# Dilated convolution on one core: which eight image rows go through four DMA engines alone

## The chip, the core and the metric

The kernel runs on one core of one Trainium2 chip. The core has a matrix engine (TensorE, "PE" in the profile, with its weight loads as "PEld"), a vector engine (VectorE, "DVE"), a scalar engine (ScalarE, "ACT"), GpSimd ("POOL") and a sync engine ("SP"). All data moves between the chip's main memory and the on-chip memory (128 partitions) through 16 DMA engines; in this kernel every transfer is issued from SP's queue. The metric is the device time of one execution in microseconds (us). Of several executions the median is taken: 126.56 us before the change, of 3 runs from 126.53 to 126.76.

## The reference

A 3x3 convolution with dilation 2 and padding 2 over 16 images of 64 channels and 64x64 pixels, giving 128 channels:

```python
batch, c_in, h, w, c_out, k, dilation = 16, 64, 64, 64, 128, 3, 2
x_pad = np.pad(x, ((0, 0), (0, 0), (pad, pad), (pad, pad)), mode='constant')   # pad = 2
for kh in range(k):
    for kw in range(k):
        output[b, co] += weight[co, ci, kh, kw] * x_pad[b, ci, kh*dilation:kh*dilation+h, kw*dilation:kw*dilation+w]
```

Input and output are float32: 16.8 MB come in and 33.6 MB go out.

## The kernel before

**Tiling.** Two images make a pair: their 2 x 64 input channels fill the 128 partitions, and there are 8 pairs. A pair is worked on in four groups of 16 image rows (`GR`), so that the main loop runs over 32 groups, `G` = 0 to 31, with `pb` the pair and `g` the group in it. The output of a pair stands in a ring of three slots (`o_ring`, L69): in a slot, partition = output channel, and then 64 rows of 64 pixels for image 0 of the pair (`m` = 0) and the same for image 1.

**Arithmetic of a group.** Input rows are cast to float16 (L83, L85), and adjacent row blocks are added (L95). Row sums, even blocks and odd blocks go through TensorE into psP, psA and psB (L186). ScalarE copies psP out of the accumulators (L248); VectorE adds it to psA and to psB and writes the result to the ring (L254). Once the second of these adds is through, all 16 rows of the group are in the ring for both images.

**Loads and stores, in SP's order.** SP issues everything itself, one transfer after the other, and each DMA engine takes its share of them in that order:

- weights; pair 0 in two pieces; pairs 1 and 2; all before the loop;
- at the end of group 0: the load of pair 3 (the fourth load, L65), and behind it the early store of the top rows of image 0 (L267 before);
- at the end of group 2 the load of pair 4, of group 3 that of pair 5, and then the two stores of pair 0, one for each image (`pair_store`, L205). As the top rows of image 0 are out by then, the store of image 0 begins below them;
- after group 7 the stores of pair 1 and the load of pair 6, after group 11 the stores of pair 2 and the load of pair 7, and then for each pair its two stores of 64 rows;
- the last pair is stored in halves of 32 rows, after its second and its fourth group (L268 to L275). There the first half of image 1 is cut into 24 rows, and 8 rows more (`ROWS4` = 8).

**How a store falls on the engines.** A store of all 128 partitions runs on all 16 engines, 8 partitions each. The list `FOUR` (L210) cuts one into a store of partitions 0 to 123 and one of partitions 124 to 127. Of those two the trace holds four landing counts each, where a store of 128 partitions has 16: each of them runs on four engines, with 31 partitions and one partition per engine. In the text these are "the four engines", the lowest-numbered of the 16 by the change's own name.

**What waits for transfers.** A cast waits for the load of its rows. A load waits until the casts are through with the buffer that it overwrites (three buffers, L63). VectorE's first add of a pair waits until the stores of the pair three before it have left the ring slot.

Of the kernel before, what the change touches and what calls it, by code (L numbers as in the profile page):

```python
# [10 lines left out]
def kernel(  # L11
# [24 lines left out]
    GR = 16  # L36
# [25 lines left out]
    def load(pb, cuts=(0, H)):  # L62
        x32_tiles[pb] = fpool.tile([P, HW], f32, tag="x32", name="x32")  # L63
        for lo, hi in zip(cuts[:-1], cuts[1:]):
            nc.sync.dma_start(  # L65
                out=x32_tiles[pb][:, lo * W : hi * W], in_=x_pair[pb, :, lo * W : hi * W]
            )
# [3 lines left out]
    def o_pair(pb):  # L71
        at = pb % OB * 2 * HW
        return o_ring[:, at : at + 2 * HW]
# [13 lines left out]
    def rowsum(c):  # L87
        pb, g = divmod(c, NG)
        if g == 0:
            xs_tiles[pb] = sxpool.tile([P, HW // 2], f16, tag="xs", name="xs")  # L90
        v = x16_tiles[pb][:, g * GR * W : (g + 1) * GR * W].rearrange(
            "p (b e q) -> p b e q", e=2, q=2 * W
        )
        s = xs_tiles[pb][:, g * NH : (g + 1) * NH].rearrange("p (b q) -> p b q", q=2 * W)
        nc.vector.tensor_tensor(out=s, in0=v[:, :, 0], in1=v[:, :, 1], op=add)  # L95
# [76 lines left out]
    def casts(G):  # L172
        for c, eng in CASTS.get(G, ()):
            cast(c, eng)

    def product(ps, src, kind, blk0, nblk, first, last):
        for j in (1, 0, 2):
            dw = (j - 1) * d
            o0, o1 = max(0, -dw), W - max(0, dw)
            t = kind * KW + j  # L180
            for hb in range(2):
                pp = slice(hb * CI, (hb + 1) * CI)
                rhs = src(pp, dw + o0, dw + o1)
                po = ps[:, hb * NH + blk0 * 2 * W : hb * NH + (blk0 + nblk) * 2 * W]
                po = po.rearrange("p (r w) -> p r w", w=W)[:, :, o0:o1]
                nc.tensor.matmul(  # L186
                    out=po,
                    lhsT=w_sb[pp, t * CO : (t + 1) * CO],
                    rhs=rhs,
                    start=first and j == 1,  # L190
                    stop=last and j == 2,
                )

    def blocks(x16, b0, n, e):
        v = x16.rearrange("p (b e r w) -> p b e r w", e=2, r=2, w=W)
        return lambda pp, c0, c1: v[pp, b0 : b0 + n, e, :, c0:c1]

    def store(pb, m, r0=0, r1=H, rows=((0, P),)):
        for lo, hi in rows:
            nc.sync.dma_start(  # L200
                out=out_img[2 * pb + m, lo:hi, r0 * W : r1 * W],
                in_=o_pair(pb)[lo:hi, m * HW + r0 * W : m * HW + r1 * W],
            )

    def pair_store(pb):  # L205
        for m in range(2):
            store(pb, m, GR // 4 if pb == m == 0 else 0)

    LOADS = {0: (3,), 2: (4,), 3: (5,), 7: (6,), 11: (7,)}
    FOUR = ((0, P - 4), (P - 4, P))  # L210
    ROWS4 = 8

    for G in range(ngroups):
        pb, g = divmod(G, NG)
        x16 = x16_tiles[pb]
        xs = xs_tiles[pb].rearrange("p (r w) -> p r w", w=W)
        o = o_pair(pb).rearrange("p (m b e q) -> p m b e q", m=2, e=2, q=2 * W)
        b0 = g * NBLK

        def summed():  # L220
            ps = ppool.tile([P, 2 * NH], f32, tag="p", name="psP")
            sv = lambda pp, c0, c1: xs[pp, g * GR // 2 : (g + 1) * GR // 2, c0:c1]
            product(ps, sv, 0, 0, NBLK, True, True)
            return ps

        def even():
            ps = apool.tile([P, 2 * NH], f32, tag="ab", name="psA")
            product(ps, blocks(x16, b0, NBLK, 1), 1, 0, NBLK, True, False)
            z = 1 if g == 0 else 0
            product(ps, blocks(x16, b0 + z - 1, NBLK - z, 1), 2, z, NBLK - z, False, True)  # L230
            return ps

        def odd():
            ps = apool.tile([P, 2 * NH], f32, tag="ab", name="psB")
            product(ps, blocks(x16, b0, NBLK, 0), 3, 0, NBLK, True, False)
            z = 1 if g == NG - 1 else 0
            product(ps, blocks(x16, b0 + 1, NBLK - z, 0), 4, 0, NBLK - z, False, True)
            return ps

        if G == 0:  # L240
            psA, psP, psB = even(), summed(), odd()
        else:
            psP, psA, psB = summed(), even(), odd()

        if not G:
            casts(-1)
        p_sb = spool.tile([P, 2 * NH], f32, tag="psb", name="p_sb")
        nc.scalar.copy(out=p_sb, in_=psP)  # L248
        casts(G)
        if G + 1 < ngroups:  # L250
            rowsum(G + 1)
        pv = p_sb.rearrange("p (m b q) -> p m b q", m=2, q=2 * W)
        for e, ps in ((0, psA), (1, psB)):
            nc.vector.tensor_tensor(  # L254
                out=o[:, :, b0 : b0 + NBLK, e],
                in0=ps.rearrange("p (m b q) -> p m b q", m=2, q=2 * W),
                in1=pv,
                op=add,
            )

        later = pb in (1, 2)
        if g == NG - 1 and later:
            pair_store(pb)
        for q in LOADS.get(G, ()):
            load(q)
        if G == 0:
            store(0, 0, 0, GR // 4)  # L267
        if pb == npairs - 1:  # L268
            if g % 2 == 1:
                store(pb, 0, (g - 1) * GR, (g + 1) * GR)  # L270
                if g == 1:
                    store(pb, 1, 0, 2 * GR - ROWS4)
                    store(pb, 1, 2 * GR - ROWS4, 2 * GR, FOUR)
                else:
                    store(pb, 1, (g - 1) * GR, (g + 1) * GR)  # L275
        elif g == NG - 1 and not later:
            pair_store(pb)

# [34 lines left out]
```

## Time and profile before

| | us |
|---|---|
| median of 3 runs | 126.56 |
| the profiled execution, its own time | 126.87 |
| its span, first to last instruction | 125.1 |
| TensorE busy in the span | 105.5 |
| VectorE busy | 90.4 |
| ScalarE busy | 61.2 |
| end of VectorE's last add | 108.8 |
| issue of the last store, from SP | 109.2 |
| mean DMA rate over the span | 406 GB/s |

The profiled execution is a run of its own, with 1.8 us outside its span, and it took 0.31 us more than the median. Engine times are sums over the span, and engines overlap. The slices of the page are fortieths of the span, 3.13 us each; a digit of 9 in the DMA row means that the 16 DMA engines were busy for 90% or more of that slice. "us to landing" is the time from a transfer's issue to the moment at which its semaphore has counted all of its data, waiting in the queue included.

### The profile page before, as it was taken

The page shows a single profiled execution, that of the slowest core. Times are in us where ns is not written, and L with a number is a line of the kernel's source. Part 1 is how long each engine was busy: PE and PEld are TensorE (multiplying, and loading weights), DVE is VectorE, ACT ScalarE, POOL GpSimd, SP SyncE. Part 2 cuts the span into 40 slices and gives each one's busy share as a digit, 9 for nine tenths or more (in the row PEclk, how much of TensorE's full clock was granted, in tenths as well). Part 3 has the DMA queues.
Part 4 walks back from the last instruction along what each step waited for, and adds up shares of the span by engine and source line. Part 5 has one row for each costly group of instructions (what it writes and reads, how often), then busy time and mean ns, then how long its engine had stood idle before and what let it go on. Part 6 is the DMA issues. An engine that isn't in the chain of part 4 may idle for free.

```text
span 125.1 us, 2341 instructions
## 1 busy us (share of the span) xinstructions
PE 105.5 (84%) x1000; PEld 56.6 (45%) x1000; DVE 90.4 (72%) x103; ACT 61.2 (49%) x64; POOL 6.1 (5%) x12
## 2 busy tenths in 40 slices
PE   6999999989999999999999999999999999300000
PEld 2355555535555555555555555555555555100000
DVE  0566969859998889888988898888988887700000
ACT  4279597396666666666336665666533333000000
POOL 2402306000000000000000000000000000000000
PEclk9999999999999999999999999999999999995555
DMA  4999999999999999999999999999999999999991
GB/s 136 376 447 440 440 419 424 419 440 419 287 419 436 424 430 440 411 424 445 424 422 430 424 419 445 430 424 424 435 430 414 435 440 424 424 419 411 430 390 63
DMA packets 4322, 50.78 MB, mean 406 GB/s; under 512 B 472, under 2 KB 600, under 8 KB 1112
## 3 DMA queue, kind: packets, MB, share of 16 engines
q1 hardware_dynamic: 4312, 50.63, 96.6%
q8 instruction: 8, 0.13, 0.4%
q14 instruction: 2, 0.02, 0.0%
HBM read 17.07 MB, written 33.55 MB: 405 GB/s over the span
## 4 chain that ended last, share of the span: by engine, by line
PE 64%; DVE 1%; DVEq 1%; issue 0%
PE psA L186 26%; PE psB L186 25%; PE psP L186 13%; DVE osb L254 1%; DVEq L308 1%; DVEq L254 0%
## 5 line engine op out<-in xcount | busy, mean ns | idle before, releaser
L186 PEld LDWEIGHTS <-w_sb 64*128 64x128 f16 x960 | 54.3, 94 | 45.6 <-issue 1.0
L248 ACT COPY p_sb<-psP 128x1024 f32<-128x1024 f32 x32 | 32.4, 1011 | 36.1 <-issue 18.6
L254 DVE TENSOR_TENSOR osb<-psA,p_sb 128x1024 f32<-128x1024 f32 x32 | 39.2, 1224 | 13.4 <-PE psA L186 7.6
L186 PE MATMUL psA<-x,w_sb 64*128 64x496 f16 (+3 forms) x384 | 45.1, 365 | 0.1
L186 PE MATMUL psB<-x,w_sb 64*128 64x496 f16 (+3 forms) x384 | 45.1, 365 | 0.0
L254 DVE TENSOR_TENSOR osb<-psB,p_sb 128x1024 f32<-128x1024 f32 x32 | 39.0, 1220 | 0.0
L83 ACT CAST x<-x 128x1024 f16<-128x1024 f32 (+2 forms) x27 | 28.2, 1051 | 4.4 <-DMA x<-in_x_dram 4.4
L186 PE MATMUL psP<-xs,w_sb 64*128 64x496 f16 (+1 forms) x192 | 26.0, 372 | 0.5 <-ACT p_sb L248 0.5
L95 DVE TENSOR_TENSOR xs<-x 128x512 f16<-128x512 f16 x32 | 13.3, 416 | 0.5 <-ACT x L83 0.5
L111 PE MATMUL dm<-zero 128*128 128x512 f16 x10 | 4.6, 580 | 1.2 <-DVE zero L103 1.2
L85 POOL CAST x<-x 128x896 f16<-128x896 f32 (+1 forms) x4 | 3.9, 987 | 12.5 <-DMA x<-in_x_dram 12.5
L111 PEld LDWEIGHTS <-zero 128*128 128x128 f16 x10 | 1.1, 124 | 2.7 <-issue 1.4
L121 DVE CAST wd<-w 128x192 f16<-128x192 f32 x1 | 0.5, 505 | 2.4 <-DMA w<-in_weight_dram 2.4
L134 PEld LDWEIGHTS <-wd 128*64 128x64 f16 x30 | 1.3, 140 | 2.1 <-DVE wd L121 1.1
L134 PE MATMUL wt<-ident,wd 128*64 128x128 f16 x30 | 1.9, 278 | 0.2 <-DVE wd L121 0.2
L123 ACT ACT_TABLE_LOAD x1 | 1.3, 1283 | 0.7 <-PEq L294 0.7
L146 ACT CAST w_sb<-wt 128x384 f16<-128x384 f32 x1 | 0.5, 478 | 2.0 <-PE wt L134 2.0
L148 DVE CAST w_sb<-wt 128x384 f16<-128x384 f32 x1 | 0.6, 558 | 1.2 <-PE wt L134 1.2
L123 ACT CAST wd<-w 128x192 f16<-128x192 f32 x1 | 0.5, 538 | 1.5 <-DMA w<-in_weight_dram 1.5
L122 POOL TENSOR_TENSOR wd<-w 128x192 f16<-128x192 f32 x1 | 0.8, 796 | 2.3 <-DMA w<-in_weight_dram 2.3
L103 DVE MEMSET zero<- 128x256 uint32 x1 | 0.3, 272 | 0.9 <-PEq L294 0.9
L125 POOL CAST wd<-w 128x192 f16<-128x192 f32 x1 | 0.8, 800 | 0.0
(12 smaller groups left out, 4.4 us busy)
## 6 DMA issues: line engine op xcount, KB each, us to landing
out_dram<-osb SPq DMA_DIRECT2D x13, 2048.0 KB, 20.6
x<-in_x_dram SPq DMA_DIRECT2D x7, 2048.0 KB, 14.8
out_dram<-osb SPq DMA_DIRECT2D x3, 1024.0 KB, 14.9
out_dram<-osb SPq DMA_DIRECT2D x1, 1920.0 KB, 19.0
x<-in_x_dram SPq DMA_DIRECT2D x1, 1088.0 KB, 5.5
x<-in_x_dram SPq DMA_DIRECT2D x1, 960.0 KB, 7.4
out_dram<-osb SPq DMA_DIRECT2D x1, 768.0 KB, 16.4
w<-in_weight_dram SPq DMA_DIRECT2D x1, 288.0 KB, 2.8
```

The lines of the kernel that those rows point to most:

```text
L83: eng.copy(out=out, in_=in_)
L85: eng.tensor_copy(out=out, in_=in_)
L95: nc.vector.tensor_tensor(out=s, in0=v[:, :, 0], in1=v[:, :, 1], op=add)
L111: nc.tensor.matmul(out=dm[:, 0:512], lhsT=zero[:, 0:P], rhs=zero)
L122: nc.gpsimd.tensor_tensor(out=wdv[:, 3], in0=wv[:, 0], in1=wv[:, 1], op=sub)
L123: nc.scalar.copy(out=wdv[:, 2], in_=wv[:, 0])
L125: nc.gpsimd.tensor_copy(out=wdv[:, 4], in_=wv[:, 2])
L134: nc.tensor.matmul(out=wts[k % 3][r * CI : (r + 1) * CI, c0 + j * CO : c0 + (j + 1) * CO], lhsT=wd[:, t * CI : (t + 1) * CI], rhs=ident,)
L186: nc.tensor.matmul(out=po, lhsT=w_sb[pp, t * CO : (t + 1) * CO], rhs=rhs, start=first and j == 1, stop=last and j == 2,)
L248: nc.scalar.copy(out=p_sb, in_=psP)
L254: nc.vector.tensor_tensor(out=o[:, :, b0 : b0 + NBLK, e], in0=ps.rearrange("p (m b q) -> p m b q", m=2, q=2 * W), in1=pv, op=add,)
L308: with _tile.TileContext(nc) as tc:
```

## The change

The four-engine store of eight rows moves from the end of the kernel to its beginning. Before, the four rows at the top of image 0 of pair 0 were stored early over all 16 engines, and the eight rows 24 to 31 of image 1 of the last pair went through the four engines. After, eight rows at the top of image 0 are stored early, through the four engines, in SP's order behind the load of pair 3. The late store of image 0 of pair 0 begins at row 8 and not at row 4 (56 rows instead of 60), and the first half of image 1 of the last pair is one store of 32 rows over all 16 engines. The kernel issues one DMA fewer.

```diff
     def pair_store(pb):
         for m in range(2):
-            store(pb, m, GR // 4 if pb == m == 0 else 0)
+            store(pb, m, ROWS4 if pb == m == 0 else 0)
 
     LOADS = {0: (3,), 2: (4,), 3: (5,), 7: (6,), 11: (7,)}
     FOUR = ((0, P - 4), (P - 4, P))
...
         for q in LOADS.get(G, ()):
             load(q)
         if G == 0:
-            store(0, 0, 0, GR // 4)
+            store(0, 0, 0, ROWS4, FOUR)
         if pb == npairs - 1:
             if g % 2 == 1:
                 store(pb, 0, (g - 1) * GR, (g + 1) * GR)
-                if g == 1:
-                    store(pb, 1, 0, 2 * GR - ROWS4)
-                    store(pb, 1, 2 * GR - ROWS4, 2 * GR, FOUR)
-                else:
-                    store(pb, 1, (g - 1) * GR, (g + 1) * GR)
+                store(pb, 1, (g - 1) * GR, (g + 1) * GR)
```

## The prediction, on record before the result

> **What bounds the kernel now.** I read the DMA row of the forty slices first, then the stretches at the end, then the list of DMA issues, and last who waits for transfers. From the page:
>
> ```profile
> span 125.1 us, 2341 instructions
> ...
> DMA  4999999999999999999999999999999999999991
> GB/s 136 376 447 440 440 419 424 419 440 419 287 419 436 424 430 440 411 424 445 424 422 430 424 419 445 430 424 424 435 430 414 435 440 424 424 419 411 430 390 63
> ...
> out_dram<-osb SPq DMA_DIRECT2D x13, 2048.0 KB, 20.6
> ...
> out_dram<-osb SPq DMA_DIRECT2D x1, 1920.0 KB, 19.0
> ...
> out_dram<-osb SPq DMA_DIRECT2D x1, 768.0 KB, 16.4
> ```
>
> The DMA engines are at 9 from the second slice to the last but one, some 15 us beyond VectorE's last add (108.8 us). A store waits 16 to 21 us between issue and landing, against about 5 us in which 2 MB move at 428 GB/s: the rest is waiting behind earlier transfers. So the queues never run dry, and the end is that of the DMA engine with the most to do. The page's chain of waits ends in TensorE and VectorE and is of no use here. One slice, the 11th, shows 287 GB/s at a busy share of 9.
>
> The stretches around that slice and at the end (columns: busy us of five engines, granted clock, DMA share, GB/s):
>
> ```profile
> 31.00:34.00 3.00, 3.00 (x34) 1.69 (x31) 2.91 (x4) 1.84 (x3) 0.00 (x0) 1.00 0.98 292
> ...
> 115.00:120.00 5.00, 0.00 (x0) 0.00 (x0) 0.00 (x0) 0.00 (x0) 0.00 (x0) 0.50 1.02 425
> 120.00:122.00 2.00, 0.00 (x0) 0.00 (x0) 0.00 (x0) 0.00 (x0) 0.00 (x0) 0.50 0.87 369
> 122.00:123.00 1.00, 0.00 (x0) 0.00 (x0) 0.00 (x0) 0.00 (x0) 0.00 (x0) 0.50 0.37 156
> 123.00:124.00 1.00, 0.00 (x0) 0.00 (x0) 0.00 (x0) 0.00 (x0) 0.00 (x0) 0.50 0.10 41
> ```
>
> The engines stop one by one: at 122 to 123 us a share of 0.37 is six of 16, a us later one or two. The trace's single landing counts give each engine's end (us from the span's start). After the 24-row store of the last pair, the four engines' chains are told by the small stores that only they have, and followed by their steps of 2.35 and 2.45 us they end at 123.3, 123.5, 123.8 and 124.2. The other twelve end at 120.9 to 123.3, but for one at 124.26. So the four, with their extra rows, and one straggler end almost together; the last is 0.09 us behind the last of the four. Through the middle of the run the four are among the early ones in every store.
>
> Who waits for transfers, SP's and VectorE's rows of the timeline and ScalarE's:
>
> ```profile
> 12.91 0.35 SPq L200 DMA_DIRECT2D out_dram<-osb  x1
> 17.83 4.22 SPq L65 DMA_DIRECT2D x<-in_x_dram  x2
> 34.85 1.16 ACT L83 CAST x<-x 128x1152 f16<-128x1152 f32 x1
> 84.98 1.22 DVE L254 TENSOR_TENSOR osb<-psA,p_sb 128x1024 f32<-128x1024 f32 x1 [0.58 <-DMA out_dram<-osb]
> 107.59 1.21 DVE L254 TENSOR_TENSOR osb<-psB,p_sb 128x1024 f32<-128x1024 f32 x1
> 108.83 0.95 SPq L200 DMA_DIRECT2D out_dram<-osb  x2
> ```
>
> The early store is issued at 12.91 us; SP's next work is at 17.83. Only one wait for a store to leave the ring is seen, 0.58 us before the seventh pair's first add.
>
> **The change, part by part.** The sum is one of packets on each engine, since nothing else is on the path. The trace has every packet: 1,024 B take 46 ns, 2,048 B 84, 6,144 B 234, 8,192 B 309, 15,360 B 573, 16,384 B 611. A store over all partitions is eight packets on each engine, and the small stores of the four engines are 31 + 1 packets of 2,048 B.
>
> *The twelve other engines.* Removed: the early four rows, 8 x 46 = 0.37 us. Shortened: image 0 of pair 0 from 15,360 to 14,336 B per packet; by proportion (an estimate from the 573 row) 535 ns, so 8 x 38 = 0.30 less. Lengthened: 24 rows to 32, 8 x (309 - 234) = 0.60 more. Sum -0.07 us.
>
> *The four engines.* Before: 0.37 + 8 x 573 + 8 x 234 + 32 x 84 = 0.37 + 4.58 + 1.87 + 2.69 = 9.51 us. After: 2.69 + 8 x 535 + 8 x 309 = 2.69 + 4.28 + 2.47 = 9.44. Also -0.07. The eight rows cost the same 2.69 us wherever they stand in the order.
>
> *One DMA fewer on every engine's queue.* Its fixed cost is bounded by two rows. The four-row, 128 KB store landed 0.36 to 0.40 us after the load ahead of it, which is its packets' 0.37: no fixed cost. The 8 KB store of four partitions landed 0.19 us behind the 124-row store with a packet of 84 ns: 0.1 at most, and the next step is 0.1 shorter than its like (2.35 for 2.45), so it is given back. I take 0 to -0.1, and 0. The Trainium skill, page DMA: Bandwidth & Descriptors, section Latency and other measured facts, puts a tiny transfer's round trip at no less than about 800 ns; if queued transfers paid that one after the other, the sum would be -0.87. The 0.19 says that a queue hides it.
>
> *SP.* Early, two issues instead of one: 0.35 us more at 12.91, hidden in the 4.6 us before the next load; the last pair issues two fewer by 109 us, which nothing waits for. Semaphores are used in turn over eight, and every transfer eight places back has landed before its successor is issued, with one place shifted too (nearest: the last half of image 0, issued at 108.83, behind one landed at 100.0).
>
> *What arrives later.* Between the two ends of the run the four engines are behind by 2.69 - 0.37 = 2.3 us, and by 2.0 once the first store has given back 0.30; the twelve are ahead by 0.37 and 0.67. Behind the early store stand the loads of pairs 4 and 5. Pair 4's load landed at 29.9 us and is cast from 34.85: 4.9 us of room, at most 2.3 used. For the ring slot at 84.98, the store's slowest engine was a straggler, the four were 1.7 to 2.5 ahead of it; with 2.0 added they come between 0.5 before and 0.3 behind its old time, so that the 0.58 us stays or grows to 0.9. If this cover were gone, VectorE and TensorE would stop for up to 2.0 us, and the last add would move from 108.8 to 110.8. The first engine needs the last stores at 116.0: 7 us of cover remain. The same page, section Rules for kernel authors, speaks against the change: a transfer confined to few engines is to be avoided, and one 128-partition transfer is better than two over parts. By that rule the loads behind are late; but both kernels hold the same pair of small stores, and the rows above pay for the place.
>
> Sum: -0.07 us on every engine, so on whichever is last. Profiled execution: 126.87 - 0.07 = 126.80; the median stands 0.31 below that execution, so 126.49. That is 0.06% off. A measurement of this kernel can tell about 0.2%, or 0.25 us, from no change.
>
> **The rivals.**
>
> *Slower: the four engines become the only last ones.* What packets lose beyond their sizes is not a fixed sum: between 31 and 34 us all engines lose time, on average 3 x (428 - 292)/428 = 0.95 us, single packets from 0.1 to 1.2. Being 2 us out of step with the twelve, the four may meet that stretch, or the mixed loads and stores, at a worse place. They have 0.09 us before they are last and need 0.34 more than now for 0.25 on the time. With 0.5 more: 126.49 - 0.09 + 0.5 = 126.9; with 1.0, 127.4. Small packets beside loads do not speak for it: the 128 early ones of 1,024 B took 46 to 48 ns each.
>
> *Slower: an instruction fetch falls to one of the four.* Eight fetches of 16 KB ride on the same engines (the page's q8), apparently on others than the four, and put their engine behind by at least one 611 ns packet: 126.49 - 0.09 + 0.61 = 127.0. Against it: their order should not depend on the change.
>
> *Slower: lateness reaches the arithmetic and then the queue.* It decides only from 7 us on, against 2.0 at most; with 8 us it would be 127.5.
>
> *Faster: the slow stretch at 31 us goes away.* It strikes while all engines read pair 5 nearly in step. If four out of step break it, all gain up to 0.95: 125.5; half, 126.0. Nothing shows its cause, and no other load has it.
>
> *Faster: the removed DMA has a fixed cost after all.* With four times the 0.1 bound, 126.1. The 0.37 row speaks against it. By the skill's 800 ns it would be 125.7.
>
> **How the numbers follow.** No change, 126.49 (own range 126.3 to 126.8): 0.48. Four engines last, 126.9: 0.20. Fetch, 127.0: 0.05. Lateness, 127.5: 0.03. Stretch broken, 126.0: 0.17. Fixed cost, 126.1: 0.07. Faster by over 0.2% is thus 0.24, the same 0.48, slower 0.28. A range from 126.0 to 127.0 leaves out the better half of the broken stretch (0.08), the worse third of the four-last case (0.07) and the lateness: under 0.2.
>
> **What would show it.** Right: 512 B to 2 KB packets gone (128 of 1,024 B), still 128 packets of 2,048 B, now near 25 us; the landing of pair 4's load spread by some 2.5 us instead of 1.7; casts and VectorE at the same times within 0.5 us; the four engines in the late half of every store until the end, and at the end the same staircase from 0.9 to 0.1 between 120 and 124 us. Wrong: the slice at 31 us at another rate; an engine out of work before 115 us; a staircase that is longer, with four steps of it together (a share of 0.25), or a steep one.

## The result, and the profile after

The changed kernel is slower: 127.35 us (median, 127.31 to 127.52) against 126.66 for the kernel before on the same chip, ratio 1.0057 with a 95% interval of 1.0040 to 1.0074. That is 0.69 us more, where 0.07 less was forecast, and outside the range of 126.0 to 127.0. The profiled execution after took 127.35 us, just the median; that of before, at 126.87, lies 0.21 us above its median, so the two traces show only 0.48 us of the difference (spans of 125.1 and 125.6 us).

The rows of the page after that answer to those shown of before:

```profile
span 125.6 us, 2341 instructions
...
DMA  4999999999999999999999999999999999999981
GB/s 136 384 451 428 428 423 428 415 431 386 310 439 415 449 444 418 420 423 418 444 446 412 428 433 418 438 428 423 433 428 418 433 438 423 428 418 418 428 339 57
DMA packets 4178, 50.78 MB, mean 404 GB/s; under 512 B 456, under 2 KB 456, under 8 KB 840
```

The DMA engines are busy throughout, as before, and the slow slice at 31 us is still there (310 GB/s). The counts show the edit itself: no packets between 512 B and 2 KB are left. The stretches, with the same columns as above:

```profile
31.00:34.00 3.00, 3.00 (x32) 1.69 (x30) 2.91 (x4) 1.84 (x3) 0.00 (x0) 1.00 0.89 282
...
115.00:120.00 5.00, 0.00 (x0) 0.00 (x0) 0.00 (x0) 0.00 (x0) 0.00 (x0) 0.50 1.01 428
120.00:122.00 2.00, 0.00 (x0) 0.00 (x0) 0.00 (x0) 0.00 (x0) 0.00 (x0) 0.50 0.83 352
122.00:123.00 1.00, 0.00 (x0) 0.00 (x0) 0.00 (x0) 0.00 (x0) 0.00 (x0) 0.50 0.33 139
123.00:124.00 1.00, 0.00 (x0) 0.00 (x0) 0.00 (x0) 0.00 (x0) 0.00 (x0) 0.50 0.23 98
```

The staircase at the end has changed its shape. From 120 to 123 us a little less is left to do (0.83 and 0.33 for 0.87 and 0.37), but from 123 to 124 us the share is 0.23 for 0.10: nearly four engines of 16 are still at work together. That was the sign named beforehand for a wrong forecast.

VectorE, ScalarE and SP, from the timeline after:

```profile
12.76 0.70 SPq L200 DMA_DIRECT2D out_dram<-osb  x2
17.72 4.56 SPq L65 DMA_DIRECT2D x<-in_x_dram  x2
34.75 1.16 ACT L83 CAST x<-x 128x1152 f16<-128x1152 f32 x1
85.75 1.22 DVE L254 TENSOR_TENSOR osb<-psA,p_sb 128x1024 f32<-128x1024 f32 x1 [1.46 <-PE psB L186]
107.48 1.22 DVE L254 TENSOR_TENSOR osb<-psB,p_sb 128x1024 f32<-128x1024 f32 x1
108.72 0.84 SPq L200 DMA_DIRECT2D out_dram<-osb  x2
```

The arithmetic is where it was: pair 4's cast at 34.75 us, the last add at 107.48, the last stores issued at 108.72. The one wait for the ring is longer, and its add begins at 85.75 instead of 84.98. The row names TensorE as the releaser, but the store that had to leave the slot counts its last landing at 85.63 us, on the four engines. The wait costs nothing: the last add is no later.

**Which engine, and where.** The trace has start, length and size of every packet, and on one engine the next packet starts within 4 ns of the end of the last. So the packets can be strung to 16 chains, one for each engine, and each chain's excess over the usual length of its packets can be read load by load. The four engines ended their data at 122.94, 123.08, 123.38 and 123.78 us before, and at 123.58, 123.71, 124.03 and 124.27 after: 0.60 us later on average. The other twelve, put in order, ended level or up to 0.5 us earlier, but for the one slow engine, last of them at 123.73 and 123.83. So the four are the last ones now. (The prediction's times are landings, which come 0.32 us after the data on the four and 0.46 on the slow engine; by them the slow one was last before.)

They fell behind early. At the start of the first large store the four were 2.9 us later than before, not the forecast 2.0, and the twelve 0.4 earlier. The excess lies at the end of the fourth load (pair 3), directly ahead of the small stores. On the four engines its last two packets took 1149 and 815, 968 and 858, 665 and 733, and 611 and 769 ns instead of 611 each, and on the last two engines three small packets took 212 to 318 ns instead of 84. Summed by engine that is 0.74, 0.60, 0.60 and 0.29 us, 0.56 on average: 0.42 in the load and 0.14 in the small packets. No other engine had such packets there. The four were not yet out of step when they lost it: they had begun this load at 18.07 us on average, the twelve at 18.06. As a rate it stands in one stretch, first of the kernel before, then after:

```profile
21.50:23.50 2.00, 2.00 (x24) 1.13 (x22) 1.65 (x3) 1.06 (x2) 0.00 (x1) 1.00 1.05 429
```

```profile
21.50:23.50 2.00, 2.00 (x22) 1.16 (x20) 1.34 (x3) 1.26 (x2) 0.20 (x1) 1.00 0.98 394
```

Of 429 GB/s 35 are missing over 2 us, 70 KB, or 2.6 us of one engine (a 16 KB packet takes 0.611 us): the sum over the four, 2.23 us, within the coarseness of such a stretch.

### The profile page after: what moved, and what is told of

It is laid out like the page before. It is cut to its first block, busy times and chain, and to the rows that moved or that the text cites. A ratio compares the mean times of both kernels' runs of the same rounds, so it can differ in the third digit from the quotient of the medians.

```text
span 125.6 us, 2341 instructions
## 1 busy us (share of the span) xinstructions
PE 105.4 (84%) x1000; PEld 56.4 (45%) x1000; DVE 90.0 (72%) x103; ACT 61.3 (49%) x64; POOL 6.1 (5%) x12
## 4 chain that ended last, share of the span: by engine, by line
PE 63%; DVE 1%; DVEq 1%; issue 0%
PE psA L186 26%; PE psB L186 24%; PE psP L186 13%; DVE osb L254 1%; DVEq L304 1%; DVEq L254 0%
```

## The experiments

"The string" is the run of 31 + 1 small packets on each of the four engines. Edits are against the changed kernel unless the text says otherwise. Ratios are to the kernel before, with 95% intervals.

**Does it matter that a load stands ahead, or that SP is issuing?** The string one load later:

```diff
-        if G == 0:
+        if G == 2:
             store(0, 0, 0, ROWS4, FOUR)
```

> The small stores move from behind the fourth load to behind the fifth (pair 4), at about 28 us, when SP issues nothing. Turn theory (packets of a load that stand directly ahead of the four engines' string of 32 small store packets take longer, as the last two packets of the fourth load did, 0.2 to 0.8 us over 611 ns each): the four lose 0.5 to 0.6 us again, now at the end of the fifth load, and the time is that of the changed kernel, 127.2 to 127.4. Issue theory (the loss came because SP issued the load of pair 5 and two stores at 22 us, just then): no loss at 28 us, 126.5 to 126.7. Displacement theory (the four lose wherever they are out of step with the twelve while loads and stores mix): 127.2 to 127.4.

Measured: 127.16 us, 1.0046 (1.0022 to 1.0070). The loss has moved with the string. The load of pair 4, now directly ahead of it, took 1.11 us longer on the four and 0.01 on the twelve; the load of pair 3 lost nothing. The stretch in which it ends:

```profile
25.00:28.00 3.00, 2.61 (x27) 1.23 (x23) 1.73 (x4) 3.00 (x4) 0.00 (x0) 1.00 1.02 393
```

A busy share of 1.02 moved 425 GB/s at 115 to 120 us of the kernel before, here 393. SP issues nothing from 23.2 to 34.5 us, so an issue at the same time is not needed for the loss, and the issue theory falls as the cause at this place. Part of the loss came back: the next load, of pair 5, which loses 0.7 to 1.2 us on all engines in most of these kernels (it is the slow slice at 31 us), lost 0.40 on the four.

**The string behind the sixth load, with stores behind it:**

```diff
-        if G == 0:
+        if G == 3:
             store(0, 0, 0, ROWS4, FOUR)
```

> The small stores stand behind the load of pair 5 and ahead of the two large stores of pair 0, at about 34 us: a load ahead, but a store behind. Turn theory: loss at the end of that load, 127.1 to 127.4. If it is the way back from the small stores to a load that costs, no loss: 126.5 to 126.7. Issue theory: SP issues two stores and a load at 34.6 to 36.3 us, so a loss is possible, 126.6 to 127.3. Displacement theory: 127.1 to 127.4.

Measured: 127.51 us, 1.0062 (1.0035 to 1.0090). Here the load ahead loses no more than it does anyway (0.67 on the four, 0.71 on the twelve). But the next load in the queue, pair 6, four large stores later, lost 0.48 on the four and 0.18 on the twelve, where it loses 0.02 and 0.05 in the kernel before.

**The string between two large stores:**

```diff
             store(pb, m, ROWS4 if pb == m == 0 else 0)
+            if pb == m == 0:
+                store(0, 0, 0, ROWS4, FOUR)
...
-        if G == 0:
-            store(0, 0, 0, ROWS4, FOUR)
```

> The small stores stand between the two large stores of pair 0, at about 38 us: a store ahead and a store behind, as at the end of the run in the kernel before, but still early and with loads to come. Turn theory: no loss, the four engines' 31 + 1 packets take 2.57 us as in the last pair, and the time is that of the kernel before less 0.07, 126.4 to 126.7. Displacement theory: 127.1 to 127.4. Issue theory: 126.5 to 126.7.

Measured: 127.34 us, 1.0052 (1.0033 to 1.0070). The turn theory fails as I had put it: the string itself took 2.49 + 0.09 us, just as in the last pair of the kernel before, nothing was lost around it, and the time came out slow all the same. The loss is in the load of pair 6 again, three large stores later: 0.61 us on the four, 0.23 on the twelve.

**SP's later issues, moved by one group in the program:**

```diff
-    LOADS = {0: (3,), 2: (4,), 3: (5,), 7: (6,), 11: (7,)}
+    LOADS = {0: (3,), 2: (4,), 4: (5,), 7: (6,), 11: (7,)}
...
+        if G == NG:
+            pair_store(0)
...
-        elif g == NG - 1 and not later:
+        elif g == NG - 1 and not later and pb:
```

> The changed kernel, with the load of pair 5 and the two stores of pair 0 issued one group later, at about 25.5 us instead of 22, so that SP issues nothing while the four engines come to the end of the fourth load and to the small stores (21.5 to 24.5 us). Turn theory: the loss of 0.5 to 0.6 us on the four stays, 127.2 to 127.4. Issue theory: it goes, 126.5 to 126.7. Displacement theory: stays.

Measured: 127.22 us, 1.0056 (1.0035 to 1.0077). The load of pair 3 lost 0.55 on the four and nothing on the twelve. But the edit did not move the issues. SP's rows, first of the changed kernel, then of this one:

```profile
21.92 0.36 SPq L65 DMA_DIRECT2D x<-in_x_dram  x1
22.33 0.90 SPq L200 DMA_DIRECT2D out_dram<-osb  x2
```

```profile
21.96 0.36 SPq L65 DMA_DIRECT2D x<-in_x_dram  x1
22.37 0.91 SPq L200 DMA_DIRECT2D out_dram<-osb  x2
```

The load and the two stores still go out at 22 us and not at 25.5: the edit changed neither their order in SP's queue nor what they wait for. So this run is the changed kernel once more and shows the loss a second time. It says nothing on the issue theory, which rests on the run with the string one load later; whether an issue at 22 us adds to the loss in the changed kernel was not tested.

So the new theory was: what an early string costs, loads pay, and behind the last load it is free.

**The string behind the last load, and ahead of it.** The first of two kernels stores the rows of pair 3 so, at about 80 us; the second has 2 for 3 and stores those of pair 2, at about 63 us. Neither has an early store.

```diff
-            store(pb, m, ROWS4 if pb == m == 0 else 0)
+            cut = pb == 3 and m == 0
+            store(pb, m, ROWS4 if cut else 0)
+            if cut:
+                store(pb, m, 0, ROWS4, FOUR)
...
-        if G == 0:
-            store(0, 0, 0, ROWS4, FOUR)
```

> The four engines' eight rows are those at the top of image 0 of pair 3, stored between the two large stores of that pair, at about 80 us: still 40 us before the end, but behind the last load (which lands at about 75 us). No early store at all. Load theory (what the four lose when their extra rows come early is lost in loads, which run slower while the four are out of step; the small stores themselves take 2.57 us everywhere): no load is left, so no loss, 126.4 to 126.7. Displacement theory as first put (out of step costs wherever it is): 127.1 to 127.4.

Measured: 126.80 us, 1.0005 (0.9992 to 1.0018).

> The same with the rows of pair 2, at about 63 us, ahead of the last load (pair 7). Load theory: that load loses 0.4 to 0.6 us on the four and 0.2 on the others, as the load of pair 6 did when the small stores stood between the stores of pair 0: 126.9 to 127.3. If only the first turn from loads to stores (pairs 3 to 6) is touchy: 126.4 to 126.7.

Measured: 127.66 us, 1.0074 (1.0056 to 1.0091). One move of the same string by one pair makes 0.9 us. The last load runs from about 68 to 75 us. Its middle, from 70 to 74, in the kernel before, the changed one, the kernel with the string behind the last load, and the one with the string ahead of it:

```profile
70.00:74.00 4.00, 4.00 (x44) 2.27 (x40) 3.84 (x5) 1.96 (x2) 0.00 (x0) 1.00 1.03 438
```

```profile
70.00:74.00 4.00, 4.00 (x44) 2.24 (x41) 3.84 (x5) 2.00 (x3) 0.00 (x0) 1.00 1.03 442
```

```profile
70.00:74.00 4.00, 4.00 (x44) 2.24 (x42) 3.84 (x5) 1.98 (x3) 0.00 (x0) 1.00 1.02 436
```

```profile
70.00:74.00 4.00, 4.00 (x44) 2.23 (x41) 3.84 (x5) 2.00 (x3) 0.00 (x0) 1.00 1.03 365
```

The share stays at 1.03, the rate falls from 436 to 365 GB/s: the engines are at work on packets that take longer. By the chains that load lost 0.94 us on the four and 0.67 on the twelve, though on the twelve this kernel differs from the one with the string behind the last load only in the sizes of two stores.

**Small early packets, or four engines?** The kernel before, with eight rows early on all 16 engines, and its string left in the last pair:

```diff
-            store(pb, m, GR // 4 if pb == m == 0 else 0)
+            store(pb, m, GR // 2 if pb == m == 0 else 0)
...
-            store(0, 0, 0, GR // 4)
+            store(0, 0, 0, GR // 2)
```

> The kernel before, with eight rows instead of four in the early store, on all 16 engines, and the four engines' rows left in the last pair. If small early packets of 2,048 B are the cause, whatever engines they run on: up to 0.4 us lost at the end of the fourth load, 126.8 to 127.2. If four engines being out of step is the cause: 126.5 to 126.7.

Measured: 126.68 us, 0.9995 (0.9986 to 1.0004). The same eight rows, as early and in packets of the same size, cost no time when spread. Yet the load ahead lost 0.17 us on all engines: summed over 16 that is 2.7 us, and the changed kernel's loss summed over the four is 2.2. The kernel without any string, further down, shows the same at this place, 0.15 us on each engine. So small packets behind this load do cost it something, on any engines; what the four engines add is that the loss falls on them alone. Here each engine lost little, and pair 5's load happened to lose only about half its usual 1.0. Four engines also differ from sixteen in the partitions that one engine serves (31 for 8); no run varies that alone.

**Are the four the last ones?**

```diff
-    ROWS4 = 8
+    ROWS4 = 6
```

> The changed kernel with six rows instead of eight for the four engines. That takes 2 x 0.32 = 0.64 us from the four and puts 2 x 0.08 = 0.16 on all engines. If the four are the last ones in the changed kernel: 126.8 to 127.1, then set by the one slow engine among the others. If they are not: 127.4 to 127.6.

Measured: 127.03 us, 1.0027 (1.0017 to 1.0036). Yes: 0.3 us less than with eight rows, by giving them less. The four now end at 123.05 to 123.58 us, and the slow engine among the twelve is last at 123.97. The loss did not shrink with the string, though: the load of pair 3 lost 0.93 us on the four, more than with eight rows, and pair 5's 0.45, less than there (0.83).

**What is the string worth?** The changed kernel with the early rows on all 16 engines and no string at all:

```diff
-            store(0, 0, 0, ROWS4, FOUR)
+            store(0, 0, 0, ROWS4)
```

> The changed kernel, with the eight early rows on all 16 engines: no small stores on the four anywhere. The eight rows then cost every engine 8 x 84 = 0.67 us, 0.6 more than the other twelve had, and the four lose 2.57 less. By the ends of the engines the one slow engine among the twelve is last, some 0.5 us later than in the kernel before: 127.1 to 127.3, so that the changed kernel has lost about all that the four engines' rows are worth. If the even split is as good as the kernel before: 126.5 to 126.7.

Measured: 127.38 us, against 126.83 for the kernel before in the same group of runs: 1.0030 (1.0002 to 1.0059). The slow engine is last at 124.17 us, as expected. The changed kernel, at 1.0057 (1.0040 to 1.0074), is no better than the even split, so an early string is worth nothing that could be seen, where a late one is worth about 0.4 us by the ratio and 0.55 by the medians.

**The early store alone taken out**, in the kernel before:

```diff
-            store(pb, m, GR // 4 if pb == m == 0 else 0)
+            store(pb, m)
...
-        if G == 0:
-            store(0, 0, 0, GR // 4)
```

> The kernel before without its early store of four rows: image 0 of pair 0 is stored whole. One part of the change alone (rows leave the early store and the first DMA is gone). By packets 8 x 46 less and 8 x 38 more, -0.07 us: 126.5 to 126.7. If the early store itself prevents something later: 126.9 and more.

Measured: 126.83 us, 0.9994 (0.9969 to 1.0018): no difference that could be seen, with a wide interval. It is not the loss of the old early store that made the changed kernel slow.

**Half the string early**, from the kernel before:

```diff
-            store(0, 0, 0, GR // 4)
+            store(0, 0, 0, GR // 4, FOUR)
...
-    ROWS4 = 8
+    ROWS4 = 4
```

> The four engines' rows are split: four rows early behind the fourth load, four rows in the last pair. If the loss at the load ahead goes with the length of the string of small stores: 0.3 us on the four, 126.8 to 127.0. If each string costs the same whatever its length: 0.55 us, 127.1 to 127.3. No loss: 126.5 to 126.7.

Measured: 127.76 us, 1.0052 (1.0024 to 1.0081). The load ahead lost 0.35 on the four, against 0.42 and 0.55 in the two runs with the whole string there. But the load of pair 5 lost 1.21 on the four and 0.91 to 1.0 on the twelve, so that both loads together cost the four some 0.6 more than the twelve. The loss does not simply go with the length; half a string early is no better than a whole one.

**A try at a better kernel**, from the one before: five rows for the four, and 16 rows of the last store cut so that one engine has none of them.

```diff
-    ROWS4 = 8
+    ROWS4 = 5
+    FIFTEEN = ((0, P - 8), (P - 8, P))
...
-                    store(pb, 1, (g - 1) * GR, (g + 1) * GR)
+                    store(pb, 1, (g - 1) * GR, g * GR, FIFTEEN)
+                    store(pb, 1, g * GR, (g + 1) * GR)
```

> A try at a better kernel, from the one before: five rows instead of eight for the four engines in the last pair, and 16 rows of the last store as 120 and 8 partitions, which 15 and 8 engines carry. If the slow engine of the twelve (its store of 64 rows takes 5.12 us, the others' 4.86) is the sixteenth, it is relieved by 1.2 us and the four by 0.7 on balance: 126.0 to 126.3. If it is another, it gets 0.24 to 0.4 more and is last: 126.9 to 127.2.

Measured: 127.63 us, 1.0048 (1.0017 to 1.0078). It failed, and not cleanly: single packets of 4,096 B, of which the cut store and the last one consist, took up to 587 ns instead of 159 between 119.8 and 122.4 us, a loss that neither case had foreseen. Which engine is the slow one stays open. No kernel tried here beats the one before.

**Which loads lose?** In the changed kernel the last load lost nothing, though the four begin it 3.2 us behind the middle one of the twelve; with the string just ahead it lost much, with the four 2.4 us behind. So perhaps the lag decides. The kernel with the string in pair 2, with six and with ten rows:

```diff
-    ROWS4 = 8
+    ROWS4 = 6
```

> The small stores between the two large stores of pair 2, as in the run before the last load, but six rows: the four engines are 2.0 us behind the twelve at the last load, not 2.6. Lag theory (a load loses where four engines are about 2.6 us, or four of its eight packets, behind): the last load takes 4.86 us on nearly every engine, and the time is 126.6 to 126.9. First-load theory (the first load behind the small stores loses whatever the lag): it takes 5.4 to 5.8 us, 127.2 to 127.6.

Measured: 127.55 us, 1.0059 (1.0038 to 1.0080), with a loss in the last load of 1.22 us on the four and 0.91 on the twelve.

> The same with ten rows: the four are 3.2 us behind at the last load. The four have 0.64 us more to store than with eight rows, so that they are last. Lag theory: no loss in the last load, 127.1 to 127.4. First-load theory: the loss of 0.7 to 0.9 us stays, 127.9 to 128.3.

Measured: 128.00 us, 1.0090 (1.0067 to 1.0112), with 0.69 on the four and 0.75 on the twelve. The same stretch, six rows and then ten:

```profile
70.00:74.00 4.00, 4.00 (x44) 2.24 (x40) 3.84 (x5) 2.01 (x3) 0.00 (x0) 1.00 0.98 324
```

```profile
70.00:74.00 4.00, 4.00 (x44) 2.31 (x42) 3.79 (x5) 2.02 (x3) 0.00 (x0) 1.00 0.98 348
```

324 and 348 GB/s, with the four 1.9 and 3.5 us behind: the lag theory falls. The changed kernel with six rows agrees: there the four come to the last load 2.4 us behind, and it loses nothing. What all places have in common:

| the string stands | load that lost beyond the usual | the four, us | the twelve, us | ratio |
|---|---|---|---|---|
| in the last pair (before) | none | | | 1 |
| behind the load of pair 3 (the change) | pair 3, directly ahead | 0.56 | 0 | 1.0057 |
| behind the load of pair 4 | pair 4, directly ahead | 1.11 | 0.01 | 1.0046 |
| behind the load of pair 5 | pair 6, the next | 0.48 | 0.18 | 1.0062 |
| between the stores of pair 0 | pair 6, the next | 0.61 | 0.23 | 1.0052 |
| between the stores of pair 2 | pair 7, the next | 0.94 | 0.67 | 1.0074 |
| between the stores of pair 3 | none, no load follows | | | 1.0005 |

(The 0.56 holds the 0.14 lost in small packets. An instruction fetch on one engine puts up to 0.05 into a mean of the twelve, or 0.09 where it falls on one of the four.) A string that stands between loads makes one load near it slow: the one directly ahead, or else the next one behind. Behind the last load it makes none slow. How large the loss is does not follow from the length of the string or from the lag. Why a load's packets take longer near it was not found: the trace shows longer packets, not what they wait for.

## Why the prediction was wrong

- **Packets by engine.** The sums of -0.07 us held. The twelve came to the first large store 0.4 us early (0.37 forecast), and the three that end first ended 0.2 to 0.5 us sooner. The string took 2.57 us (2.49 + 0.09) at the end of the kernel before; 2.69 was 5% high, on both sides of the sum. Early it took 2.57 on two of the four engines and 2.70 and 3.01 on the others.
- **The step that failed** is the sentence "The eight rows cost the same 2.69 us wherever they stand in the order". At an early place a load near the string takes longer, and some of the string's own packets too: 0.42 + 0.14 = 0.56 us on the four, measured, and the four ended 0.60 later. The last of the four ended level with the slow engine before the change and is the last of all after it, so the time went with the four. The term was missing from the sum, since I bounded the cost of small packets beside loads by the packets themselves (46 to 48 ns each) and not by what the loads next to them did.
- **One DMA fewer** at 0 to -0.1 us: nothing in the runs contradicts it; the kernel without the early store came out at 0.9994, with an interval too wide to tell 0.1 us.
- **SP:** the second early issue took 0.35 us (0.70 for both) and was hidden, as forecast. No run moved SP's other issues.
- **Lateness:** right in kind. Pair 4's load landed between 27.8 and 31.3 us, a spread of 3.5 and not 2.5, again by the loss, and was cast at 34.75 as before. The ring's wait made the add 0.8 us later, not 0.3 at most; the last add did not move.
- **The rival that came true** is the four engines becoming the only last ones, with a chance of 0.20. It had the right place (early, loads beside stores) and a price of 0.5 us on the four, 126.9, with 127.4 for 1.0. The four lost 0.56 and ended 0.60 later. Its reason was another: the four were to meet a worse place because they were out of step, but they lost the time ahead of the string, in step. So that its price came near is in part luck. The rest of the way to 127.35 is no mechanism: the forecast took 0.31 us off to come from the profiled execution to the median, while the changed kernel's profiled execution took just its median. A range up to that rival's upper price would have held the result; its upper third was left out.
- **The other rivals:** no 16 KB fetch fell to the four, in either kernel. The stretch at 31 us stayed (282 GB/s for 292). A fixed cost of a DMA did not show.
- **The rule against the change.** The Trainium skill, page DMA: Bandwidth & Descriptors, section Rules for kernel authors, would have all 16 engines in every transfer. For a place among loads the runs agree with it only in part: eight early rows on 16 engines cost nothing where the string was left at the end (0.9995), but with no string at the end 16 engines (1.0030, interval up to 1.0059) and four (1.0057, interval from 1.0040) can't be told apart. For a place behind the last load they don't agree: a string there was as fast as the kernel before, and no string at all was 0.3% slower.

## What to carry to other kernels

Equal bytes on each DMA engine were not equal time here: the uneven store that balances the engines at the end belonged behind the last load, since at five places among loads it slowed one of them, on the engines concerned and sometimes on all. When a transfer is moved in the order, price its neighbours too, by the packet lengths of the transfers ahead and behind, and not only its own packets. Where a few engines end within 0.1 us of the last, a forecast of "no change" hangs on nothing being lost on them, and the range must say so.

## What the runs showed of the hardware

- The load of pair 5, which ends the first run of loads, loses about 1.0 us on all engines in the kernel before (means of about 0.9 on the four and 1.1 on the twelve), and between 0.4 and 1.2 in all others. This is the slow slice at 31 us. The loads of pairs 6 and 7, which stand between stores, lose next to nothing there. The cause is open.
- Each 16 KB instruction fetch makes one engine's transfer 1.3 us longer (6.18 us for a 64-row store of 4.86), more than the 0.611 us that I had put as its least price, and the eight fetches fall on eight different engines, none of them the four.
- One of the other twelve engines takes 5.1 us for most 64-row stores, the rest 4.86, in nearly every store from pair 0 to pair 6, while its loads are as fast as theirs. It adds up to some 3 us and makes this engine one of the last in nearly every kernel here.
